# Routing of a mixture of experts, computed for each tile of 128 tokens by itself

## The chip, the core and the metric

The kernel runs on one core of a Trainium2 chip. The metric is device microseconds of that core for one execution; three executions of the kernel before are known, and one further execution was profiled. TensorE (PE) does the matmuls, VectorE (DVE) and ScalarE (ACT) the elementwise work, GpSimd (POOL) a little of it, and SyncE (SP) issues the loads. Each engine takes its instructions in the order in which the program lists them for it, and waits on semaphores for the others.

## What is computed

Two transformer layers over 256 tokens of width 1024, in float32. The change lies in the mixture of experts at the end of the second one. In the notation of the reference:

- the layer's output `x` is normed (`rms_norm`), then two routers give 8 group logits and 64 expert logits per token, each with a bias;
- the group with the largest logit is chosen, and in it the two experts with the largest logits; a token's weights are the softmax of the two, times the softmax probability of the group;
- each expert (64 of them, 256 hidden units: gate, up and down matrices) is applied to the tokens that chose it, and the weighted results are added to `x`.

## The kernel before

The 256 tokens lie in two tiles `t` of 128 (a token on each of 128 partitions). Instructions are written in Python; a scheduler then sets each engine's order by priority and by when it supposes that operands will be ready, and adds the semaphores. `streams` and `on` give a block of code a priority of its own: "route" ahead of "late".

**The end of the mixers.** `accum_end` (calls L946 for `x`) finishes `x[:, 0]`, then `x[:, 1]`, and calls `then(0)` shortly before the last matmuls of tile 1 and `then(1)` behind them. `then(t)` (L1687) squares and sums each half of x on ScalarE (L1694, into `q4`), transposes x on TensorE (`hT`, L1699, L1701), and splits x into `xhi` (ScalarE, L1704) and the remainder `xlo` (VectorE, L1685). `logits(t)` multiplies `hT` by the router's weights into `ps[0]`, 72 columns per tile: tile 0's logits are issued in `then(1)`, tile 1's at its end. Behind both, `rstd2` (L420 to L433) computes the norm factors `rs` of both tiles as one [128, 2] operand, and L1718, L1719 make the logits `lg` and `le`.

**The choice.** `route` (L1737) works on both tiles at once, with operands of 16 or 128 elements per partition: `first_max` (L1730 to L1734) three times for group, first and second expert, one-hot matrices `rA` and `rB` (L1757, L1759), whose matmuls with a triangular and an all-ones matrix count, for each token, how many tokens before it chose the same expert; `rk` (L1768) is this rank. From it `expert_gather` makes the 0/1 matrices S (L1816), and 32 matmuls of S with `xhi` and `xlo` gather the tokens of eight experts into `xT` (L1833, L1834). `weigh` (L1770) computes the weights behind that.

**Fillers.** `keep_warm` (L1658) issues WARM = 22 matmuls of two constants (shown as `mm<-negcr,identr`) behind tile 1's logits, at the priority "late"; their result is not used.

**Memory banks.** The matmuls' results lie in banks of PSUM, held by pools. The pool "ps1" of the mixers is closed (`psum.close()`, L1584) and "ps4" opened (L1586) ahead of `route`: the banks of the logits belong to the first, those of the fillers, of the ranks and of the experts to the second.

**The experts.** `moe` (L1914) goes through 16 groups of four experts. The weights come in 1 MB tiles into a ring of 16 buffers; `first_weights` (L1898) issues the first loads, before the routing, and `expert_ahead` (L1868) issues one whenever a buffer is freed, all from SP (L1883).

Of the kernel before, what the change touches and what calls it, by code (L numbers as in the profile page):

```python
# [149 lines left out]
class Kern:  # L150
# [1514 lines left out]
    def router_logits(self, x):  # L1665
# [6 lines left out]
        lg = self.T(16, "lg").rearrange("p (t g) -> p t g", t=2)  # L1672
        le = self.T(128, "le").rearrange("p (t e) -> p t e", t=2)
        q4 = self.T(4, "n4q4")
        rs, hr = (self.ph.tile([128, 2], F, name=k) for k in ("n4rs", "n4hr"))
        ps = []

        def logits(t):
            for k in range(8):
# [6 lines left out]

        def then(t):  # L1687
            if t == 0:
                ps.append(self.bank("sm"))
            else:  # L1690
                logits(0)
            for i in range(2):
                junk = self.T(512, "junk")
                nc.scalar.activation(junk, x[:, t, i * 512:i * 512 + 512], AF.Square, accum_out=q4[:, 2 * t + i:2 * t + i + 1])  # L1694
# [19 lines left out]
            logits(1)  # L1714
            for t in range(2):
                r = rs[:, t:t + 1]
                v = ps[0][:, t * 72:t * 72 + 72]
                nc.vector.scalar_tensor_tensor(lg[:, t], v[:, 0:8], r, self.b["b_router_group_2"], op0=OP.mult, op1=OP.add)  # L1718
                nc.vector.scalar_tensor_tensor(le[:, t], v[:, 8:72], r, self.b["b_router_expert_2"], op0=OP.mult, op1=OP.add)  # L1719
        self.rs4, self.hr4 = rs, hr  # L1720
        return (lg, le), (hi, lo), then

    def first_max(self, v, name):

        nc = self.nc
        mx, m2 = self.T(2, name + "m"), self.T(2, name + "n")
        e = self.T(16, name + "e").rearrange("p (t g) -> p t g", t=2)
        oh = self.T(16, name + "o").rearrange("p (t g) -> p t g", t=2)
        b = lambda t: t[:, :, None].to_broadcast([128, 2, 8])
        nc.vector.tensor_reduce(mx, v, axis=AX.X, op=OP.max)  # L1730
        for t in range(2):
            nc.vector.scalar_tensor_tensor(e[:, t], v[:, t], mx[:, t:t + 1], self.c["desc"], op0=OP.is_equal, op1=OP.mult)
        nc.vector.tensor_reduce(m2, e, axis=AX.X, op=OP.max)
        nc.vector.tensor_tensor(oh, e, b(m2), op=OP.is_equal)  # L1734
        return oh, mx

    def route(self, lg, le):  # L1737

        nc, c, mm = self.nc, self.c, self.nc.tensor.matmul
        b = lambda t, n=8: t[:, :, None].to_broadcast([128, 2, n])  # L1740
        f = lambda t: t.rearrange("p t g -> p (t g)")
        with self.on("late"):
            self.keep_warm(WARM, self.logit)
        ohg, mg = self.first_max(lg, "fg")
        d = self.T(16, "rd").rearrange("p (t g) -> p t g", t=2)
        nc.vector.tensor_tensor(d, lg, b(mg), op=OP.subtract)
        g4 = ohg[:, :, :, None].to_broadcast([128, 2, 8, 8])
        e4 = lambda t: t[:, :, None, :].to_broadcast([128, 2, 8, 8])
        v4 = lambda t: t.rearrange("p (t g e) -> p t g e", t=2, g=8)
        tmp = self.T(128, "rt")  # L1750
        nc.vector.tensor_tensor(v4(tmp), le.rearrange("p t (g e) -> p t g e", g=8), g4, op=OP.mult)
        el = self.T(16, "el").rearrange("p (t e) -> p t e", t=2)
        nc.vector.tensor_reduce(el, v4(tmp).rearrange("p t g e -> p t e g"), axis=AX.X, op=OP.add)
        o1, v1 = self.first_max(el, "f1")
        nc.vector.scalar_tensor_tensor(el, o1, BIG, el, op0=OP.mult, op1=OP.add)
        A1, A2 = self.T(128, "rA"), self.T(128, "rB")
        nc.vector.tensor_tensor(v4(A1), g4, e4(o1), op=OP.mult)  # L1757
        o2, v2 = self.first_max(el, "f2")
        nc.vector.tensor_tensor(v4(A2), g4, e4(o2), op=OP.mult)  # L1759
        self.rk = self.gs.tile([128, 2, 64], F, name="rk")  # L1760
        p = self.bank()
        for A in (A1, A2):
            mm(p[:, 0:128], c["stri"], A, start=A is A1, stop=False)
            mm(p[:, 64:128], c["ones"], A[:, 0:64], start=False, stop=A is A2)
        nc.vector.tensor_tensor(A1, A1, A2, op=OP.add)
        self.low()
        rk = self.rk.rearrange("p t e -> p (t e)")
        nc.vector.scalar_tensor_tensor(rk, p[:, :128], 1.0, A1, op0=OP.add, op1=OP.mult)  # L1768

        def weigh():  # L1770

            self.W = self.gs.tile([128, 2, 64], F, name="rW")
            e2, w1, pg = self.T(2, "e2"), self.T(2, "w1"), self.T(2, "pg")
            w = self.T(16, "aw").rearrange("p (t e) -> p t e", t=2)
# [3 lines left out]
            nc.vector.tensor_reduce(pg, d, axis=AX.X, op=OP.add)  # L1778
# [4 lines left out]
            nc.vector.tensor_tensor(w1, w1, self.rs4, op=OP.mult)  # L1783
# [356 lines left out]
```

## Time and profile before

| | us |
|---|---|
| median of three executions | 1461.39 (1459.74 to 1462.12) |
| the profiled execution, its own time | 1462.19 |
| its span in the profile | 1460.4 |
| TensorE busy | 1385.0 (95%) |
| VectorE busy | 864.1 (59%) |
| ScalarE busy | 588.9 (40%) |
| weight loads, mean over the span | 233 GB/s |

The span is counted from the first to the last instruction of the profiled execution; 1.8 us of its time lie around it. Engine shares are means over stages of different kind: the mixers and the first layer up to about 980 us, the routing from about 980 to 1001, and the experts from there. Rows of the timeline carry the start in the span, the busy time, the engine, the line, the operation, the tiles written and read, the size and the number of like instructions.

### The profile page before, as it was taken

The page shows a single profiled execution, that of the slowest core. Times are in us where ns is not written, and L with a number is a line of the kernel's source. Part 1 is how long each engine was busy: PE and PEld are TensorE (multiplying, and loading weights), DVE is VectorE, ACT ScalarE, POOL GpSimd, SP SyncE. Part 2 cuts the span into 40 slices and gives each one's busy share as a digit, 9 for nine tenths or more (in the row PEclk, how much of TensorE's full clock was granted, in tenths as well). Part 3 has the DMA queues.
Part 4 walks back from the last instruction along what each step waited for, and adds up shares of the span by engine and source line. Part 5 has one row for each costly group of instructions (what it writes and reads, how often), then busy time and mean ns, then how long its engine had stood idle before and what let it go on. Part 6 is the DMA issues. An engine that isn't in the chain of part 4 may idle for free.

```text
span 1460.4 us, 22493 instructions
## 1 busy us (share of the span) xinstructions
PE 1385.0 (95%) x9045; PEld 1052.3 (72%) x9045; DVE 864.1 (59%) x1750; ACT 588.9 (40%) x1062; POOL 91.9 (6%) x71
## 2 busy tenths in 40 slices
PE   7999999999999999899999999999999999999996
PEld 6989998999899999688798899985434333333321
DVE  7788686567788778588868886873213113112212
ACT  5546655544555556355664664451111001101100
POOL 0110202020011111200000000000000000000000
PEclk9999999999999999899999999998999999999999
DMA  8413423433555556433345345497999999999996
GB/s 272 146 60 118 145 75 104 154 107 124 191 170 182 196 178 198 124 117 115 103 130 172 90 142 173 149 388 322 422 421 421 421 421 420 421 421 420 421 421 274
DMA packets 132010, 341.32 MB, mean 234 GB/s; under 512 B 7872, under 2 KB 84672, under 8 KB 107840
## 3 DMA queue, kind: packets, MB, share of 16 engines
q1 hardware_dynamic: 131904, 339.86, 62.6%
q8 instruction: 72, 1.18, 0.3%
q14 instruction: 34, 0.28, 0.1%
HBM read 338.79 MB, written 1.05 MB: 233 GB/s over the span
## 4 chain that ended last, share of the span: by engine, by line
PE 72%; DMA 12%; DVE 10%; ACT 4%; issue 1%; POOL 0%; SPq 0%; DVEq 0%; ACTq 0%; POOLq 0%
PE mm L143 45%; PE sm L143 13%; PE at L143 6%; PE dn L143 5%; DMA raw<-in_wdn 4%; DMA early<-in_wdn 3%; DMA early<-in_wgu 2%; PE sm L147 2%; DVE whl L322 2%; DMA raw<-in_wgu 1%; ACT whl L321 1%; DMA raw<-in_w_in 1%; PE at L147 1%; ACT myhi L334 1%; DMA raw<-in_w_down 0%
## 5 line engine op out<-in xcount | busy, mean ns | idle before, releaser
L322 DVE TENSOR_TENSOR whl<-raw,whl 128x1024 fp32r<-128x1024 f32 (+2 forms) x256 | 306.0, 1198 | 80.4 <-ACT whl L321 78.8
L321 ACT ACTIVATE whl<-raw 128x1024 fp32r<-128x1024 f32 (+2 forms) x256 | 262.3, 1026 | 180.6 <-PE mm L143 155.7
L143 PE MATMUL mm<-raw,xT 128*32 128x512 f32 x672 | 184.1, 595 | 5.2 <-ACT xT L1833 2.8
L143 PE MATMUL mm<-n1hi,whl 128*128 128x256 f32 (+2 forms) x880 | 173.8, 289 | 0.0
L335 DVE SCALAR_TENSOR_TENSOR mylo<-dn,wq,myhi 128x512 fp32r<-128x512 f32 x32 | 24.0, 751 | 217.3 <-ACT myhi L334 215.7
L143 PEld LDWEIGHTS mm<-n1hi,whl 128*128 128x128 f32 (+2 forms) x880 | 140.2, 190 | 0.7 <-ACT n1hi L334 0.2
L143 PE MATMUL mm<-n3hi,whl 128*128 128x256 f32 (+1 forms) x656 | 127.3, 288 | 2.4 <-DVE whl L322 1.5
L143 PE MATMUL mm<-n2hi,whl 128*128 128x256 f32 x704 | 129.5, 285 | 0.1
L143 PE MATMUL mm<-n1lo,whl 128*128 128x256 f32 (+2 forms) x440 | 125.4, 285 | 1.0 <-DVE n1lo L335 1.0
L143 PEld LDWEIGHTS mm<-n2hi,whl 128*128 128x128 f32 x704 | 111.3, 193 | 0.7 <-ACT n2hi L334 0.3
L143 PEld LDWEIGHTS mm<-n3hi,whl 128*128 128x128 f32 (+1 forms) x656 | 103.5, 189 | 5.2 <-issue 2.0
L143 PEld LDWEIGHTS mm<-raw,xT 128*32 128x32 f32 x672 | 43.1, 109 | 83.7 <-issue 71.6
L334 ACT ACTIVATE myhi<-dn,wq 128x512 fp32r<-128x512 f32 x32 | 22.0, 688 | 198.5 <-PE dn L143 198.5
L143 PE MATMUL mm<-n2lo,whl 128*128 128x256 f32 x352 | 99.8, 285 | 0.3 <-DVE n2lo L335 0.3
L143 PE MATMUL dn<-raw,mhT 128*32 128x512 f32 x384 | 92.9, 594 | 2.7 <-DMA raw<-in_wdn 2.2
L143 PE MATMUL mm<-n3lo,whl 128*128 128x256 f32 (+1 forms) x328 | 93.6, 285 | 0.0
L143 PEld LDWEIGHTS mm<-n1lo,whl 128*128 128x128 f32 (+2 forms) x440 | 83.3, 189 | 1.8 <-DVE n1lo L335 1.4
L143 PEld LDWEIGHTS dn<-raw,mhT 128*32 128x32 f32 x384 | 26.4, 110 | 61.2 <-issue 52.5
L143 PEld LDWEIGHTS mm<-n2lo,whl 128*128 128x128 f32 x352 | 67.9, 193 | 0.9 <-DVE n2lo L335 0.5
L143 PE MATMUL mm<-whl,n3hi 128*128 128x512 f32 x192 | 61.2, 396 | 2.0 <-DVE whl L322 1.5
L143 PEld LDWEIGHTS mm<-n3lo,whl 128*128 128x128 f32 (+1 forms) x328 | 62.0, 189 | 1.0 <-issue 0.7
L143 PE MATMUL mm<-early,xT 128*32 128x512 f32 x144 | 61.3, 595 | 0.0
(536 smaller groups left out, 2719.7 us busy)
## 6 DMA issues: line engine op xcount, KB each, us to landing
raw<-in_wgu SPq DMA_DIRECT2D x84, 1024.0 KB, 19.8
raw<-in_w_in SPq DMA_DIRECT2D x56, 1024.0 KB, 5.3
raw<-in_wdn SPq DMA_DIRECT2D x48, 1024.0 KB, 19.8
whl<-in_wgu SPq DMA_DIRECT2D x26, 1024.0 KB, 19.8
raw<-in_w_up SPq DMA_DIRECT2D x22, 1024.0 KB, 5.1
early<-in_wgu SPq DMA_DIRECT2D x18, 1024.0 KB, 19.8
raw<-in_w_down SPq DMA_DIRECT2D x11, 1024.0 KB, 4.8
whl<-in_wdn SPq DMA_DIRECT2D x9, 1024.0 KB, 19.8
```

The lines of the kernel that those rows point to most:

```text
L143: return self.of.matmul(out, lhsT, rhs, **k)
L147: return self.of.transpose(*a, **k)
L321: nc.scalar.activation(out[0], w, AF.Copy)
L322: nc.vector.tensor_tensor(out[1], w, out[0].bitcast(F), op=OP.subtract)
L334: nc.scalar.activation(hi, src, AF.Copy, scale=scale)
L335: nc.vector.scalar_tensor_tensor(lo, src, scale, hi.bitcast(F), op0=OP.mult, op1=OP.subtract)
```

## The change

`route` is cut in two. `scale(t)` computes the norm factor of one tile: ten operations of one element per partition, called in `then(t)`. `route_part(t)` makes the logits, the three choices, the one-hots `A1` and `A2`, their matmuls and the rank of one tile: 21 operations of VectorE with 1, 8 or 64 elements per partition and two matmuls of 64 columns, for tile 0 two more (the all-ones matrix, which adds tile 0's counts to tile 1's ranks). `route_part(0)` is called in `then(1)` right behind `logits(0)`; `route_part(1)` is kept as `route_last` and called in `route`, behind the call of `keep_warm`. The bank `p` of the rank matmuls is now taken in `then(0)`, next to that of the logits, and so from the pool "ps1". The tiles that both parts write are held in `self.rt`; `weigh` takes over the subtraction that makes `rd`.

```diff
@@ block23
-            lgs, xs, then = self.router_logits(x)
+            xs, then = self.router_logits(x)
...
             with self.on("route"):
-                weigh = self.route(*lgs)
+                weigh = self.route()
@@ router_logits
+        def scale(t):
+            r, (v, h, w) = rs[:, t:t + 1], (self.T(1, "n4" + k) for k in "vhw")
+            nc.vector.tensor_tensor(v, q4[:, 2 * t:2 * t + 1], q4[:, 2 * t + 1:2 * t + 2], op=OP.add)
+            nc.vector.tensor_scalar(v, v, 1.0 / 1024, EPS, op0=OP.mult, op1=OP.add)
+            nc.vector.tensor_scalar(r.bitcast(I32), v.bitcast(I32), -0.5, MAGIC, op0=OP.mult, op1=OP.add)
+            nc.vector.tensor_scalar(h, v, -0.5, None, op0=OP.mult)
+            for _ in range(3):
+                nc.vector.scalar_tensor_tensor(w, r, h, r, op0=OP.mult, op1=OP.mult)
+                nc.vector.scalar_tensor_tensor(r, w, 1.5, r, op0=OP.add, op1=OP.mult)
...
             if t == 0:
-                ps.append(self.bank("sm"))
+                ps.extend(self.bank("sm") for _ in range(2))
             else:
                 logits(0)
+                self.route_part(0, *ps)
...
             if t == 0:
+                scale(0)
                 low(0, 0)
                 low(0, 1)
                 return
-            ssq = self.T(2, "n4q")
-            nc.vector.tensor_tensor(ssq, q4[:, 0:4:2], q4[:, 1:4:2], op=OP.add)
-            self.rstd2(ssq, "n4", rs)
+            scale(1)
             low(1, 0)
             self.low = lambda: low(1, 1)
             logits(1)
...
+            self.route_last = lambda: self.route_part(1, *ps)
@@ first_max
+    def first_max(self, v, oh, mx, name):
...
         nc.vector.tensor_reduce(mx, v, axis=AX.X, op=OP.max)
+        nc.vector.scalar_tensor_tensor(e, v, mx, self.c["desc"], op0=OP.is_equal, op1=OP.mult)
         nc.vector.tensor_reduce(m2, e, axis=AX.X, op=OP.max)
+        nc.vector.tensor_scalar(oh, e, m2, None, op0=OP.is_equal)
...
+    def route_part(self, t, ps, p):
...
+        nc.vector.scalar_tensor_tensor(lg, v[:, 0:8], r, self.b["b_router_group_2"], op0=OP.mult, op1=OP.add)
+        nc.vector.scalar_tensor_tensor(le, v[:, 8:72], r, self.b["b_router_expert_2"], op0=OP.mult, op1=OP.add)
+        self.first_max(lg, og, z["mg"][:, t], "fg")
+        tmp, el = self.T(64, "rt"), self.T(8, "el")
+        nc.vector.tensor_tensor(v4(tmp), v4(le), g4, op=OP.mult)
+        nc.vector.tensor_reduce(el, v4(tmp).rearrange("p g e -> p e g"), axis=AX.X, op=OP.add)
+        self.first_max(el, o1, z["v1"][:, t], "f1")
+        nc.vector.scalar_tensor_tensor(el, o1, BIG, el, op0=OP.mult, op1=OP.add)
+        nc.vector.tensor_tensor(v4(A1), g4, e4(o1), op=OP.mult)
+        self.first_max(el, o2, z["v2"][:, t], "f2")
+        nc.vector.tensor_tensor(v4(A2), g4, e4(o2), op=OP.mult)
+        for i, A in enumerate((A1, A2)):
+            mm(p[:, t * 64:t * 64 + 64], c["stri"], A, start=t == 0 and i == 0, stop=i == 1)
+        if t == 0:
+            for A in (A1, A2):
+                mm(p[:, 64:128], c["ones"], A, start=A is A1, stop=False)
+        s = self.T(64, "rs")
+        nc.vector.tensor_tensor(s, A1, A2, op=OP.add)
+        nc.vector.scalar_tensor_tensor(rk, p[:, t * 64:t * 64 + 64], 1.0, s, op0=OP.add, op1=OP.mult)
...
         with self.on("late"):
             self.keep_warm(WARM, self.logit)
...
+        self.route_last()
         self.low()
```

What the scheduler makes of it on TensorE, between tile 1's logits (`sm<-rw,h2T`) and the first gather matmul (`sm<-S,xhi`). `negcr,identr` are the fillers, `rA` and `rB` the one-hot matrices (in the changed program `rA_10452` is A1 and `rA_10453` is A2, of both tiles). Before:

```order
L143 MATMUL sm<-rw,h2T 128x72 x3
L143 MATMUL mm<-negcr,identr 128x128 [waits DVE_49,PE_49]
L143 MATMUL mm<-negcr,identr 128x128 x11
L143 MATMUL sm<-rA,consts 128x128 [waits DVE_49]
L143 MATMUL sm<-rA,consts 128x64
L143 MATMUL mm<-negcr,identr 128x128 x4
L143 MATMUL sm<-rB,consts 128x128 [waits DVE_49]
L143 MATMUL sm<-rB,consts 128x64
L143 MATMUL mm<-negcr,identr 128x128 x6
L143 MATMUL sm<-S,xhi 128x256 [waits DVE_49] x2
```

And in the changed kernel:

```order
L143 MATMUL sm<-rA_10452,consts 128x64 [waits DVE_49]
L143 MATMUL sm<-rA_10453,consts 128x64 [waits DVE_49]
L143 MATMUL sm<-rA_10452,consts 128x64
L143 MATMUL sm<-rA_10453,consts 128x64
L143 MATMUL sm<-rA_10452,consts 128x64 [waits DVE_49]
L143 MATMUL sm<-rA_10453,consts 128x64 [waits DVE_49]
L143 MATMUL mm<-negcr,identr 128x128 [waits DVE_49]
L143 MATMUL mm<-negcr,identr 128x128 x21
L143 MATMUL sm<-S,xhi 128x256
L143 MATMUL sm<-S,xhi 128x256 [waits DVE_49]
```

The fillers, which stood in three pieces ahead of, between and behind the one-hot matmuls, stand in one piece behind the last of them, and the first waits for VectorE.

On VectorE, the end of the norm factors and the logits before:

```order
L946 SCALAR_TENSOR_TENSOR x<-sm,x 128x512
L1685 TENSOR_TENSOR xlo<-x,xhi 128x512
L1710 TENSOR_TENSOR n4q<-n4q_10443 128x2
L420 TENSOR_SCALAR n4v<-n4q 128x2
L427 TENSOR_SCALAR n4rs<-n4v 128x2
L428 TENSOR_SCALAR n4h<-n4v 128x2
L432 SCALAR_TENSOR_TENSOR n4t<-n4rs,n4h 128x1 x2
L433 SCALAR_TENSOR_TENSOR n4rs<-n4t,n4rs 128x2
L1685 TENSOR_TENSOR xlo<-x,xhi 128x512
```

The same place in the changed kernel, from the last x (L946) into tile 0's choice; L1683 to L1689 are `scale`, L1736 to L1739 `first_max`, L1698 is `xlo`:

```order
L946 SCALAR_TENSOR_TENSOR x<-sm,x 128x512
L1751 SCALAR_TENSOR_TENSOR rlg<-sm,n4rs,rows 128x8
L1752 SCALAR_TENSOR_TENSOR rle<-sm,n4rs,rows 128x64
L1736 TENSOR_REDUCE rmg<-rlg 128x1
L1698 TENSOR_TENSOR xlo<-x,xhi 128x512
L1737 SCALAR_TENSOR_TENSOR fge<-rlg,rmg,consts 128x8
L1738 TENSOR_REDUCE fgn<-fge 128x1
L1739 TENSOR_SCALAR rog<-fge,fgn 128x8
L1755 TENSOR_TENSOR rt<-rle,rog 128x64
L1698 TENSOR_TENSOR xlo<-x,xhi 128x512
L1756 TENSOR_REDUCE el<-rt 128x8
```

Tile 0's logits and choice follow the last x directly, with both remaining `xlo` between them. The norm factor of tile 1 (L1683 to L1689) begins sixteen operations and two `xlo` behind the first `rlg` row, among the last steps of tile 0's chain; tile 1's own `rlg` stands behind tile 0's rank and half of S.

## Rows read from the trace of the kernel before

**Rows 1.** The page's part 2, bandwidth in 40 slices of 36.5 us each.
```profile
GB/s 272 146 60 118 145 75 104 154 107 124 191 170 182 196 178 198 124 117 115 103 130 172 90 142 173 149 388 322 422 421 421 421 421 420 421 421 420 421 421 274
```

**Rows 2.** Windows: busy time per engine, granted clock, DMA share, GB/s.
```profile
998.00:1000.00 2.00, 2.00 (x11) 2.00 (x11) 0.73 (x2) 0.55 (x2) 1.01 (x2) 0.50 0.90 369
1000.00:1002.00 2.00, 2.00 (x16) 1.49 (x16) 1.05 (x4) 0.91 (x2) 0.00 (x0) 0.99 0.11 41
...
1014.00:1016.00 2.00, 2.00 (x12) 0.47 (x8) 0.00 (x0) 0.00 (x0) 0.00 (x0) 1.00 0.39 82
...
1020.00:1040.00 20.00, 20.00 (x125) 9.86 (x126) 3.52 (x8) 3.57 (x7) 1.21 (x2) 1.00 1.01 423
```

**Rows 3.** Timeline of the load queue (SP): start us, us, line, op, transfer.
```profile
982.17 0.33 SPq L1883 DMA_DIRECT2D whl<-in_wdn  x1
1005.22 0.33 SPq L1883 DMA_DIRECT2D early<-in_wdn  x1
```

**Rows 4.** Timeline of TensorE, routing and gather (PE matmul, PEld weight load).
```profile
984.18 2.21 PE L143 MATMUL sm<-rw,h2T 128*128 128x72 f32 x16 [0.25 <-ACT h2T L1701]
...
988.62 1.73 PE L143 MATMUL mm<-negcr,identr 128*128 128x128 f32 x12 [2.23 <-DVE fgm L1730]
...
991.59 1.12 PE L143 MATMUL sm<-rA,consts 128*128 128x128 f32 x4 [1.25 <-DVE rA L1757]
...
994.10 1.40 PEld L143 LDWEIGHTS mm<-negcr,identr 128*128 128x128 f32 x6
...
995.38 0.55 PEld L143 LDWEIGHTS sm<-S,xhi 128*128 128x128 f32 x2
...
995.49 0.73 PE L143 MATMUL sm<-S,xhi 128*128 128x256 f32 x2
...
996.45 0.63 PE L143 MATMUL sm<-S,xhi 128*128 128x256 f32 x2
...
996.88 0.63 PE L143 MATMUL sm<-S,xlo 128*128 128x256 f32 x2
...
1000.89 0.40 PE L143 MATMUL sm<-S,xhi 128*128 128x256 f32 x2
...
1001.13 0.40 PE L143 MATMUL sm<-S,xlo 128*128 128x256 f32 x2
...
1001.57 2.77 PE L143 MATMUL mm<-early,xT 128*32 128x512 f32 x12
```

**Rows 5.** Timeline of VectorE and ScalarE in the same stretch; [idle before <-releaser].
```profile
980.67 0.69 DVE L946 SCALAR_TENSOR_TENSOR x<-sm,x 128x512 f32<-128x512 f32 x1 [2.24 <-PE sm L143]
...
982.48 0.68 DVE L946 SCALAR_TENSOR_TENSOR x<-sm,x 128x512 f32<-128x512 f32 x1
...
984.77 0.16 DVE L1710 TENSOR_TENSOR n4q<-n4q 128x2 f32<-128x2 f32 x1 [1.00 <-ACT junk L1694]
...
985.11 0.63 ACT L1704 ACTIVATE xhi<-x 128x512 fp32r<-128x512 f32 x1
...
985.90 0.69 DVE L1685 TENSOR_TENSOR xlo<-x,xhi 128x512 fp32r<-128x512 f32 x1
986.50 0.34 DVE L432 SCALAR_TENSOR_TENSOR n4t<-n4rs,n4h 128x1 f32<-128x1 f32 x2
...
988.98 0.17 DVE L1733 TENSOR_REDUCE fgn<-fge 128x2 f32<-128x16 f32 x1
989.18 0.18 DVE L1734 TENSOR_TENSOR fgo<-fge,fgn 128x16 f32<-128x16 f32 x1
...
994.45 0.29 DVE L1768 SCALAR_TENSOR_TENSOR rk<-sm,rA 128x128 f32<-128x128 f32 x1 [1.30 <-PE sm L143]
994.77 0.76 DVE L1816 TENSOR_TENSOR S<-rk,consts 128x256 fp32r<-128x256 f32 x2
```

**Rows 6.** Windows of 0.25 us, columns as in rows 2; granted clock third from last.
```profile
989.75:990.00 0.25, 0.25 (x4) 0.25 (x3) 0.25 (x1) 0.00 (x0) 0.00 (x0) 0.58 1.28 524
...
1000.00:1000.25 0.25, 0.25 (x4) 0.25 (x3) 0.24 (x1) 0.00 (x0) 0.00 (x0) 0.94 0.16 66
```

More of the change, by code (lines that the diff above doesn't have):

```diff
@@ L1671, in router_logits @@
         hi, lo = v(self.U8("xhi", R)), v(self.U8("xlo", R))
-        lg = self.T(16, "lg").rearrange("p (t g) -> p t g", t=2)
-        le = self.T(128, "le").rearrange("p (t e) -> p t e", t=2)
         q4 = self.T(4, "n4q4")
@@ L1676, in router_logits @@
         ps = []
+        two = lambda n, name: self.ph.tile([128, 2 * n], F, name=name).rearrange("p (t g) -> p t g", t=2)
+        z = self.rt = {k: two(n, "r" + k) for k, n in (("lg", 8), ("le", 64), ("og", 8), ("o1", 8), ("o2", 8), ("mg", 1),
+                                                      ("v1", 1), ("v2", 1), ("A1", 64), ("A2", 64), ("rk", 64))}
+        self.rk = z["rk"]
+        def scale(t):
[7 more added lines that the diff above has]
+                nc.vector.scalar_tensor_tensor(r, w, 1.5, r, op0=OP.add, op1=OP.mult)
         def logits(t):
@@ L1714, in then @@
             logits(1)
[L1715 to L1719, printed above, removed]
+            self.route_last = lambda: self.route_part(1, *ps)
         self.rs4, self.hr4 = rs, hr
-        return (lg, le), (hi, lo), then
@@ L1723, in first_max @@
-    def first_max(self, v, name):
+        return (hi, lo), then
+    def first_max(self, v, oh, mx, name):
         nc = self.nc
[L1726 to L1729, printed above, removed]
+        m2, e = self.T(1, name + "n"), self.T(8, name + "e")
         nc.vector.tensor_reduce(mx, v, axis=AX.X, op=OP.max)
-        for t in range(2):
-            nc.vector.scalar_tensor_tensor(e[:, t], v[:, t], mx[:, t:t + 1], self.c["desc"], op0=OP.is_equal, op1=OP.mult)
+        nc.vector.scalar_tensor_tensor(e, v, mx, self.c["desc"], op0=OP.is_equal, op1=OP.mult)
@@ L1733, in first_max @@
         nc.vector.tensor_reduce(m2, e, axis=AX.X, op=OP.max)
[L1734 to L1740, printed above, removed]
+        nc.vector.tensor_scalar(oh, e, m2, None, op0=OP.is_equal)
+    def route_part(self, t, ps, p):
+        nc, c, mm, z = self.nc, self.c, self.nc.tensor.matmul, self.rt
+        r = self.rs4[:, t:t + 1]
+        v = ps[:, t * 72:t * 72 + 72]
+        lg, le, og, o1, o2 = (z[k][:, t] for k in ("lg", "le", "og", "o1", "o2"))
+        A1, A2, rk = (z[k][:, t] for k in ("A1", "A2", "rk"))
+        g4 = og[:, :, None].to_broadcast([128, 8, 8])
+        e4 = lambda o: o[:, None, :].to_broadcast([128, 8, 8])
+        v4 = lambda o: o.rearrange("p (g e) -> p g e", g=8)
+        nc.vector.scalar_tensor_tensor(lg, v[:, 0:8], r, self.b["b_router_group_2"], op0=OP.mult, op1=OP.add)
[17 more added lines that the diff above has]
+        nc.vector.scalar_tensor_tensor(rk, p[:, t * 64:t * 64 + 64], 1.0, s, op0=OP.add, op1=OP.mult)
@@ L1741, in route @@
+    def route(self):
+        nc, z = self.nc, self.rt
+        b = lambda t, n=8: t.to_broadcast([128, 2, n])
         f = lambda t: t.rearrange("p t g -> p (t g)")
+        g4 = z["og"][:, :, :, None].to_broadcast([128, 2, 8, 8])
+        e4 = lambda t: t[:, :, None, :].to_broadcast([128, 2, 8, 8])
+        o1, o2, v1, v2 = (z[k] for k in ("o1", "o2", "v1", "v2"))
         with self.on("late"):
             self.keep_warm(WARM, self.logit)
-        ohg, mg = self.first_max(lg, "fg")
-        d = self.T(16, "rd").rearrange("p (t g) -> p t g", t=2)
@@ L1746, in route @@
[L1746 to L1764, printed above, removed]
@@ L1765, in route @@
-        nc.vector.tensor_tensor(A1, A1, A2, op=OP.add)
+        self.route_last()
         self.low()
-        rk = self.rk.rearrange("p t e -> p (t e)")
-        nc.vector.scalar_tensor_tensor(rk, p[:, :128], 1.0, A1, op0=OP.add, op1=OP.mult)
         def weigh():
             self.W = self.gs.tile([128, 2, 64], F, name="rW")
-            e2, w1, pg = self.T(2, "e2"), self.T(2, "w1"), self.T(2, "pg")
-            w = self.T(16, "aw").rearrange("p (t e) -> p t e", t=2)
+            e2, w1, pg = (self.T(2, k).rearrange("p (t o) -> p t o", t=2) for k in ("e2", "w1", "pg"))
+            w, d = (self.T(16, k).rearrange("p (t e) -> p t e", t=2) for k in ("aw", "rd"))
+            nc.vector.tensor_tensor(d, z["lg"], b(z["mg"]), op=OP.subtract)
@@ L1777, in weigh @@
             nc.scalar.activation(e2, v2, AF.Exp)
-            nc.vector.tensor_reduce(pg, d, axis=AX.X, op=OP.add)
+            nc.vector.tensor_reduce(pg[:, :, 0], d, axis=AX.X, op=OP.add)
             nc.vector.reciprocal(pg, pg)
@@ L1782, in weigh @@
             nc.vector.tensor_tensor(w1, w1, pg, op=OP.mult)
-            nc.vector.tensor_tensor(w1, w1, self.rs4, op=OP.mult)
+            nc.vector.tensor_tensor(w1[:, :, 0], w1[:, :, 0], self.rs4, op=OP.mult)
             nc.vector.tensor_scalar(self.hr4, self.rs4, 0.5, None, op0=OP.mult)
```

## The prediction

> **What bounds the kernel now.** I read the span in slices first. From the slice that begins at 1022 us on the weight DMAs move 420 to 422 GB/s without a break [rows 1], and the window of 20 us at 1020 shows all 16 DMA engines busy, share 1.01 [rows 2]. So the last 430 us (the mixture of experts, 200 MB of expert weights) run at the pace of the weight stream, and the kernel ends a fixed time after the stream last stood still. The 2 us windows show where that is: share 0.90 at 998 and 0.11 at 1000, then a shorter rest at 1014, share 0.39 [rows 2]. The queue of weight loads shows why: the load issued at 982.17 fills the last free buffer, and the next one goes out at 1005.22, as soon as TensorE has used up the first expert tile [rows 3]. TensorE's first expert matmul starts at 1001.57 [rows 4]. **Hence the rule of the whole forecast: whatever moves the first expert matmul moves the restart of the stream, and with it the end, by the same amount**, later without limit, earlier by at most the 5 us from 1000.2 to 1005.2 in which the stream rests.
>
> Ahead of that matmul stands the routing. Tile 1's logits run on TensorE from 984.18 for 2.21 us [rows 4]; VectorE computes the norm factors for both tiles from 984.77, then the choice of groups and experts, the rank `rk` at 994.45 and the gather matrices S from 994.77 [rows 5]; the gather's matmuls start at 995.49, its last pair at 1001.13 [rows 4]. Two other things share this stretch. TensorE has little to do, so the program gives it 22 filler matmuls; in the trace 12 run from 988.62, 4 between the one-hot matmuls, 6 from 994.10, all while VectorE still works, so that they cost nothing [rows 4]. And TensorE's clock falls: half of the granted clock (1.2 of 2.4 GHz) from about 989.8 (0.58 in the window at 989.75), full again only at 1000.0 [rows 6], although TensorE was at work since 991.59 [rows 4]; the filler and one-hot matmuls of 991.6 to 995.4 did not bring it back, and it came 4.5 us after the gather had begun.
>
> **Part one: VectorE's chain.** The change makes two chains of one, each for 128 tokens. The price of a step is 0.20 us, since the 0.17 us L1733 at 988.98 is followed by its reader at 989.18 [rows 5]; halving an operation's 16 or 128 elements hardly lowers it. What matters is when tile 0's chain can run. Its first ten operations (norm factor) fall into VectorE's idle time: nine of them, 1.8 us, against an idle 2.24 us ahead of 980.67 [rows 5]. They begin only when the squares are summed, so I charge 0.3 us, by which the later x of tile 1 (issued at 982.48 and 0.68 long before [rows 5]) ends at 983.5. Tile 0's routing follows from there. One chain from `lg` to `rk` is 21 operations: 4.2 us; two are 8.4. Between them stand tile 1's ten norm operations, four of which fit into gaps of tile 0's chain, so 1.2; two `xlo` at 0.60 of issue, 1.2 (0.69 long, the next starts at 986.50 [rows 5]); the first half of S, 0.4 (half of the 0.76 of L1816 [rows 5]). The second of these `xlo` stands in the middle of tile 0's chain and needs the last `xhi`, which ScalarE ends at 985.74 [rows 5]; the chain gets there about 985.5, so 0.3 of waiting. The two ranks wait for their one-hot matmuls: the before kernel's `rk` waited 1.30 for four passes of them [rows 5], two passes of half the width are wanted now, and I take 0.4 each. Six operations need no earlier result and start 0.1 sooner: minus 0.6. Sum: 983.5 + 8.4 + 1.2 + 1.2 + 0.4 + 0.3 + 0.8 - 0.6 = 995.2. Against 994.45 **the last rank comes 0.7 us later**, not earlier; bounds 994.7 (no waits) to 995.9 (a 1.3 us wait at the second rank). The reason is plain: tile 1's sums are ready at 984.77 [rows 5], but VectorE, which takes its work in order, is with tile 0 until about 989.5.
>
> **Part two: the fillers.** TensorE also works in order, and all 22 fillers now stand between the last one-hot matmul and the gather, the first with a wait on VectorE. Their bank belongs to a pool that is opened where the old one is closed; the change leaves the last read of the old pool, tile 1's `rk`, behind that point, and the awaited count in the built program is that operation. So no filler can run while VectorE works; they all run when it is done. Their pace at half clock is 1.28 us for the six from 994.10 to the gather's first weight load at 995.38 [rows 4], 0.213 each; 22 take 4.7 us. The clock is low by then: TensorE has some six short matmuls between the logits' end at 986.39 and 995. The first filler starts at 995.2 + 0.3 (the length of `rk` and a handover), S is ready 0.4 later and hidden. **The gather starts at 995.5 + 4.7 = 1000.2, 4.7 us later than 995.49.**
>
> **Part three: the gather.** It has 32 matmuls, 0.43 a pair at half clock (996.45 to 996.88) and 0.24 a pair at full clock (1000.89 to 1001.13) [rows 4]. Before, from 995.49 to the first expert matmul at 1001.57, it took 6.1 with the clock back after 4.5 us. Where the clock returns in the new gather can't be read from the trace. If it is back 2 us into it, 9 matmuls are slow and 23 fast, 4.7 us in all and 5.0 to the first expert matmul (1.1 less than before); if it stays low to the end, 32 x 0.213 = 6.8, or 7.1 (1.0 more). I take 0.3 less, since fillers run right before it; the end at 7.1 is unlikely because the clock would have to stay low for 11 us of continuous work, against 8.4 from 991.59 to 1000.0, so I keep +0.5 as the upper end.
>
> **Part four: the rest.** The weights of the pair of experts (`weigh`) get one more subtraction in the shadow of the gather; two one-hot matmuls of 64 columns for tile 0 run while TensorE idles; ScalarE's and the load queue's orders stay; the memset of `base` moves into an early idle place. All zero: TensorE or the stream is what is waited for. If the `weigh` chain lost its cover, it would be 0.2.
>
> **Sum.** +4.7 - 0.3 = +4.4 us on the first expert matmul, bounds: rank at 994.7 and gather 1.1 shorter, +3.1; rank at 995.9 and gather 0.5 longer, +5.9. The profiled execution (span 1460.4, its own time 1462.19) would become 1466.6; it lies 0.8 above the median of the three runs, so on the median of 1461.39 the forecast is **1465.8**. About 0.2%, 2.9 us, is what a measurement of this kernel can tell from no change.
>
> **Rivals.** *A, the clock comes back during the fillers.* 22 matmuls in a row are work, too. If it returns as the gather begins, the gather takes 16 x 0.24 + 0.3 = 4.1 instead of 6.1, and the sum is +2.7: 1464.1. If it returns half-way through the fillers, 11 of them save 0.1 each: +1.6, 1463.0. Against it: 3.9 us of fillers and one-hots, from 991.59, did not do it before [rows 4, 6]. The Trainium skill speaks for it: "TensorE: Matmul & The Clock Gate", What's actually happening, says that "the default state is throttled, and activity releases the throttle". By that rule 22 unbroken matmuls would end in the full clock, and rival A's time would hold; no row of before shows such a run of fillers alone.
>
> *B, not slower: the clock does not fall at all.* If TensorE's few one-hot matmuls of tile 0, about 987.8 to 989.3, keep the clock up, the fillers take between half of 0.213 and the 1.73 / 12 = 0.144 of the twelve from 988.62 [rows 4], 2.4 to 3.2 us, and the gather 4.1: first expert matmul at 995.5 + 2.4 + 4.1 = 1002.0 to 1002.8, +0.4 to +1.2, 1461.8 to 1462.6, which is no change. It decides if the clock is full at 995.5. Against it: before, it fell at 989.8 although twelve fillers had been running since 988.62 [rows 4, 6]; now the gap is longer and emptier.
>
> *C, the stream takes the delay up.* If the restart hung on something else than the first tile's release, the delay would vanish in the stream: 0, or 1461.4. (If only the second short rest shrank, 1.2 us in the window at 1014 [rows 2], 3.2 would be left, inside the forecast's own range.) Against it: the load at 1005.22 goes out right behind TensorE's use of that tile [rows 3, 4], and that second rest comes from TensorE's steps too, so it moves along.
>
> *D, faster, as the change is meant.* If tile 0's chain were done by 984.77, tile 1's own part, ten and 21 operations or about 6.4 us, would put the rank at 991.2, 3.3 us earlier; with the fillers at half clock behind it the gather would still start at 996.2, 0.7 late. Only if the clock holds as well, as in B, does it start at 993.9 and the first expert matmul at 998.0: -3.6, 1457.8. Tile 0's x is complete on VectorE only about 983 [rows 5], so I give it little.
>
> **Chances.** Forecast 0.78; A 0.10; B 0.05; C 0.04; D 0.03. A to C lie within 0.2%, D is faster with the clock up; of the forecast's own range all lies above +2.9. So slower 0.78, same 0.19, faster 0.03. The range runs from 1463.0 (most of A is inside; B, C and D are not) to 1467.3 (+5.9); some 0.14 is left out.
>
> **What would show it.** Right: in the changed profile no filler runs between 986.5 and 995; `rk` of tile 1 ends about 995.4; 22 fillers in a row about 995.5 to 1000.2 at a granted clock of 0.50; gather from about 1000.2; first expert matmul about 1006; the stream rests about 1000 to 1010.5 and runs at 421 GB/s from there, with all later stages shifted. Wrong in part one if the last rank ends before 994; wrong in part two if fillers run at full clock or before the rank; wrong in the rule if the first expert matmul moves and the end does not.

## The result

The changed kernel takes 1467.95 us (median of 6 runs, 1465.47 to 1469.61), the kernel before 1460.38 beside it (6 runs, 1457.37 to 1462.12). The ratio is 1.0055, 95% interval 1.0044 to 1.0066: **8.0 us slower (6.4 to 9.6)**. The forecast was slower by 4.4, with a range up to 1467.3. The direction was right, the size too small.

The profiled execution took 1469.15 us with a span of 1467.4, against 1460.4 before: 7.0 us in the traces. How far a run has come when the routing begins differs from run to run (the row of VectorE that completes tile 0's `x`, L946 x2, called the last joint x here, starts at 977.06 before, 977.38 after, between 973.25 and 977.83 in the experiments), so from here on times are also given from the start of that x.

TensorE of the changed kernel, from tile 0's one-hot matmuls to the first expert matmul. Columns of a timeline: start, duration (us), engine, line, operation, output and inputs, count, and in brackets the idle time ahead and what ended it.

```profile
989.33 1.54 PE L143 MATMUL sm<-rA,consts 128*128 128x64 f32 x6 [0.62 <-DVE rA L1761]
995.22 0.69 PE L143 MATMUL sm<-rA,consts 128*128 128x64 f32 x2 [4.36 <-DVE rA L1759]
996.28 0.69 PE L143 MATMUL sm<-rA,consts 128*128 128x64 f32 x2 [0.37 <-DVE rA L1761]
997.28 4.96 PE L143 MATMUL mm<-negcr,identr 128*128 128x128 f32 x22 [0.32 <-DVE rrk L1769]
1002.04 0.73 PE L143 MATMUL sm<-S,xhi 128*128 128x256 f32 x2
...
1008.05 1.48 PE L143 MATMUL mm<-early,xT 128*32 128x512 f32 x6
```

All 22 fillers stand in one piece behind tile 1's rank and hold up the gather by 1002.04 - 997.28 = 4.76 us. It begins at 1002.04 (before 995.49), the first expert matmul at 1008.05 (1001.57) [rows 4]. VectorE, with the waits that matter:

```profile
983.68 0.22 DVE L1751 SCALAR_TENSOR_TENSOR rlg<-sm,n4rs,rows 128x8 f32<-128x8 f32 x1
...
986.09 0.69 DVE L1698 TENSOR_TENSOR xlo<-x,xhi 128x512 fp32r<-128x512 f32 x1 [0.47 <-ACT xhi L1718]
...
990.90 0.23 DVE L1769 SCALAR_TENSOR_TENSOR rrk<-sm,rs 128x64 f32<-128x64 f32 x1 [1.05 <-PE sm L143]
...
992.14 0.23 DVE L1751 SCALAR_TENSOR_TENSOR rlg<-sm,n4rs,rows 128x8 f32<-128x8 f32 x1
...
992.66 0.23 DVE L1737 SCALAR_TENSOR_TENSOR fge<-rlg,rmg,consts 128x8 f32<-128x8 f32 x1
992.92 0.16 DVE L1738 TENSOR_REDUCE fgn<-fge 128x1 f32<-128x8 f32 x1
993.12 0.23 DVE L1739 TENSOR_SCALAR rog<-fge,fgn 128x8 f32<-128x8 f32 x1
993.39 0.22 DVE L1755 TENSOR_TENSOR rt<-rle,rog 128x64 f32<-128x64 f32 x1
...
997.00 0.23 DVE L1769 SCALAR_TENSOR_TENSOR rrk<-sm,rs 128x64 f32<-128x64 f32 x1 [0.52 <-PE sm L143]
```

Tile 0's rank (the first `rrk`) waits 1.05 us for the six one-hot passes of 989.33, and tile 1's norm factor stands behind it, so tile 1's `rlg` comes only at 992.14. Tile 1's rank comes at 997.00, where `rk` stood at 994.45 [rows 5]. The queue of weight loads and the DMA engines in windows (columns: window, length, busy time of PE, PEld, DVE, ACT, POOL, granted clock, DMA share, GB/s):

```profile
982.37 0.33 SPq L1898 DMA_DIRECT2D whl<-in_wdn  x1
1011.70 0.33 SPq L1898 DMA_DIRECT2D early<-in_wdn  x1
```

```profile
1000.00:1002.00 2.00, 2.00 (x11) 2.00 (x11) 0.00 (x0) 0.00 (x0) 1.19 (x2) 0.50 0.13 53
1010.00:1012.00 2.00, 2.00 (x12) 0.53 (x10) 0.00 (x0) 0.00 (x0) 0.61 (x1) 1.00 0.00 0
1014.00:1016.00 2.00, 2.00 (x15) 1.08 (x12) 0.00 (x0) 0.27 (x1) 0.00 (x0) 1.00 1.02 430
...
989.25:989.50 0.25, 0.17 (x1) 0.18 (x2) 0.25 (x5) 0.00 (x0) 0.00 (x0) 0.65 1.18 492
...
1006.25:1006.50 0.25, 0.25 (x3) 0.25 (x3) 0.20 (x1) 0.02 (x1) 0.00 (x0) 0.71 0.00 0
```

The load that went out at 1005.22 [rows 3] now goes out at 1011.70; the stream has run dry at 1000, as before [rows 2], and rests 6.5 us longer. The clock is at half (0.50) from about 989.3 to 1006.4, through all the fillers, and returns 4.4 us after the gather began.

### The profile page after: what moved, and what is told of

Read it like the earlier page. It is cut to its first block, busy times and chain, and to the rows that moved or that the text cites. A ratio compares the mean times of both kernels' runs of the same rounds, so it can differ in the third digit from the quotient of the medians.

```text
span 1467.4 us, 22519 instructions
## 1 busy us (share of the span) xinstructions
PE 1388.0 (95%) x9049; PEld 1054.7 (72%) x9049; DVE 865.7 (59%) x1773; ACT 588.1 (40%) x1062; POOL 93.1 (6%) x71
## 3 DMA queue, kind: packets, MB, share of 16 engines
HBM read 338.79 MB, written 1.05 MB: 232 GB/s over the span
## 4 chain that ended last, share of the span: by engine, by line
PE 72%; DMA 11%; DVE 10%; ACT 4%; issue 1%; POOL 1%; SPq 0%; DVEq 0%; ACTq 0%; POOLq 0%
PE mm L143 45%; PE sm L143 14%; DMA raw<-in_wdn 7%; PE at L143 6%; PE dn L143 5%; DMA early<-in_wgu 2%; PE sm L147 2%; DVE whl L322 2%; DMA raw<-in_wgu 1%; ACT whl L321 1%; DMA raw<-in_w_in 1%; PE at L147 1%; ACT myhi L334 1%; POOL fy L1152 0%; DVE pr L478 0%
```

## The experiments

Every kernel below ran five rounds beside the kernel before. One table holds what was read from the traces (us from the start of the last joint x, one execution each; "gather lasts" is up to the first expert matmul; "restart" is the load behind the first expert tile) and the times (ratio to before times 1460).

| kernel | last rank | gather starts | gather lasts | restart | time against before, us |
|---|---|---|---|---|---|
| before | 17.39 | 18.43 | 6.08 | 28.16 | 0 |
| after | 19.62 | 24.66 | 6.01 | 34.32 | +8.0 (6.4 to 9.6) |
| e1: after, no fillers | 18.96 | 19.24 | 5.84 | 28.73 | +2.5 (1.2 to 3.8) |
| e2: after, bank of tile 1's rank from the new pool | 19.47 | 21.15 | 5.94 | 30.74 | +4.2 (2.9 to 5.5) |
| e3: before, bank of `rk` from the old pool | 16.89 | 21.99 | 6.10 | 31.74 | +3.7 (2.3 to 5.0) |
| e4: before, no fillers | 16.89 | 17.69 | 6.49 | 27.83 | -0.4 (-1.8 to +1.0) |
| e5: before, wide fillers | 16.48 | 17.29 | 4.14 | 25.08 | -2.0 (-3.4 to -0.7) |
| e6: after, tile 0's rank later | 18.82 | 23.85 | 6.35 | 33.85 | +8.6 (6.6 to 10.7) |
| e7: before, norm factor by tile | 16.63 | 17.67 | 6.04 | 27.36 | +0.3 (-1.0 to +1.6) |
| e8: e5 and e7 together | 15.71 | 16.51 | 4.13 | 24.29 | -3.5 (-5.0 to -1.9) |
| e9: e6 with 24 wide fillers | 18.57 | 18.84 | 5.56 | 28.05 | +0.7 (-1.0 to +2.3) |
| e10: e6 with 29 wide fillers | 18.59 | 18.87 | 5.63 | 28.15 | +0.3 (-1.2 to +1.8) |

Theory at the start: the loss is the fillers behind tile 1's rank plus a longer VectorE chain, and the restart of the stream hands it to the end. Rivals: the clock, or the chain alone.

**e1, the fillers out of the changed kernel.**

```diff
-            self.keep_warm(WARM, self.logit)
+            self.keep_warm(0, self.logit)
```

> The changed kernel without its 22 filler matmuls. Theory F (the loss is first of all the 22 fillers, which queue behind tile 1's rank, 4.76 us in the changed profile): the gather starts 0.5 us behind tile 1's rank, about 997.7 instead of 1002.04, and the kernel loses only the longer VectorE chain, about 2.2 us, plus up to 1.0 if the clock stays at half through the whole gather: 2.0 to 3.3 us over before. Rival K (the loss is the clock, which the fillers win back): the gather takes 7 us instead of 6 and little is gained, 5.5 us or more over before. Rival M (the program behind the routing has become slower): still 7 over before.

1462.81 us against 1460.39, ratio 1.0017 (1.0008 to 1.0026). Two rows of VectorE and the gather's first:

```profile
989.48 0.23 DVE L1769 SCALAR_TENSOR_TENSOR rrk<-sm,rs 128x64 f32<-128x64 f32 x1 [0.39 <-PE sm L143]
995.58 0.23 DVE L1769 SCALAR_TENSOR_TENSOR rrk<-sm,rs 128x64 f32<-128x64 f32 x1 [0.53 <-PE sm L143]
```

```profile
995.86 1.04 PE L143 MATMUL sm<-S,xhi 128*128 128x256 f32 x3 [0.32 <-DVE rrk L1769]
```

The gather starts 0.28 after the rank instead of 5.04, and 5.6 us of the restart's 6.2 are gone. What stays is the longer chain: the last rank comes 1.57 later than before; a gather that starts closer behind it (0.28 against 1.04) and is 0.24 shorter gives 1.0 of this back, so the restart is 0.6 late. The time is 2.5 later (1.2 to 3.8), more than the restart explains. In this execution the one-hot passes of tile 0 still fell into the full clock (0.88 for six, 1.54 in the changed kernel), so the first rank waited 0.39 and not 1.05.

**e2, the fillers set free another way.** Tile 1's rank takes its bank from the pool that is opened later; the all-ones passes move there with it. The last read of the old pool is then that of tile 1's logits, for which the fillers still wait.

```diff
+        if t == 1:
+            p = self.bank()
+            for i, A in enumerate((z["A1"][:, 0], z["A2"][:, 0])):
+                mm(p[:, 64:128], c["ones"], A, start=i == 0, stop=False)
```

> The changed kernel with tile 1's rank in a bank of the new pool, so that the fillers wait only for tile 1's logits to be read; they stand 9, 4 and 9 between the one-hot matmuls. F: the fillers are hidden again, the gather starts about 0.5 us behind tile 1's rank, and the time is 2 to 2.5 us over before. K: clock granted at half from 990 to the middle of the gather as in both kernels, no gain over the kernel without fillers. M: 7 over before. If F and K both fall short, something else holds the gather back.

1463.87, ratio 1.0029 (1.0020 to 1.0038). The fillers now run in pieces of 9, 4 and 9, the first two while VectorE works; some of the last piece still stands ahead of the gather:

```profile
992.89 2.16 PE L143 MATMUL mm<-negcr,identr 128*128 128x128 f32 x9
...
994.85 0.73 PE L143 MATMUL sm<-S,xhi 128*128 128x256 f32 x2
```

Tile 1's rank was at 993.17 and half of S had long been there, so the gather could have begun about 993.5 and began at 994.85. The wait came from the pool, and giving the last reader another bank takes most of it away (1.68 behind the rank instead of 5.04). Two things fell short of the 2 to 2.5 us that were expected: this rest of the fillers, and a second rank that waited 0.97, with fillers between its one-hot passes, where it waits 0.52 in the changed kernel.

**e3, the wait alone, in the kernel before.**

```diff
-                ps.append(self.bank("sm"))
+                ps.extend(self.bank("sm") for _ in range(2))
+                self.rank_bank = ps[1]
...
-        p = self.bank()
+        p = self.rank_bank
```

> The kernel before with one thing changed: the bank of the rank matmuls is taken from the old pool, so that all 22 fillers stand behind the rank, as in the changed kernel; VectorE's work is untouched. F: rank as before or a little earlier (its one-hot matmuls no longer share TensorE with fillers, up to 0.4), then 22 x 0.216 = 4.75 us of fillers, gather from about 999.3, 4.0 to 4.8 us over before. Rival V (VectorE's two chains are the loss): no loss here.

1462.88, ratio 1.0025 (1.0016 to 1.0034). TensorE:

```profile
993.54 4.96 PE L143 MATMUL mm<-negcr,identr 128*128 128x128 f32 x22 [0.38 <-DVE rk L1769]
998.29 0.73 PE L143 MATMUL sm<-S,xhi 128*128 128x256 f32 x2
```

The routing is that of before, word for word; where a bank comes from is enough to push all fillers behind `rk` and to cost 3.6 us at the restart and 3.7 in the time. The same 4.75 us lie between the first filler and the gather. About 0.5 of it is paid back at the rank (16.89 against 17.39), because the one-hot passes no longer share TensorE with fillers.

**e4, no fillers in the kernel before.** The edit is that of e1.

> The kernel before without fillers: what they are worth where they cost nothing. F: the gather starts as before or up to 0.4 earlier; the time is between 0.4 less and 1.0 more than before. K: the clock comes back later than at 1000.0, the gather takes 6.8 to 7.1 instead of 6.1 us, and the time is 0.7 to 1.0 more.

1460.06, ratio 0.9997 (0.9988 to 1.0007). The rank comes 0.5 earlier, the gather lasts 0.4 longer. The fillers of the kernel before gain nothing that can be measured; the clock falls and returns with or without them.

**e5, fillers that TensorE can run at once.** The narrow ones are taken out and 22 matmuls of 512 columns go behind tile 1's logits, on a bank of the old pool.

```diff
+        def hold(n):
+            p = self.bank("mm")
+            for _ in range(n):
+                nc.tensor.matmul(p[:, 0:512], self.identr, hi[:, 0, 0:512], start=True, stop=True)
...
             logits(1)
+            hold(22)
```

> The kernel before with its 22 fillers of 128 columns taken out and 22 matmuls of 512 columns put in, from a bank of the old PSUM pool, so that nothing makes them wait: two inside the second tile's logits, twenty behind them and ahead of the one-hots. They fill TensorE's idle time from the logits' end to the first one-hot, 5.3 us in the kernel before without fillers, at about 0.22 each (17 matmuls of 512 columns of the first expert took 4.05). Theory: the clock stays full when TensorE has no gap, the narrow fillers of before only come too late and too sparse. Then the four passes of each one-hot take 0.55 instead of 1.1, `rk` waits 0.3 instead of 0.81, and the gather takes 4.1 to 4.5 instead of 6.08 to 6.49: 1.5 to 2.5 us faster than before. Rival: the clock falls whatever stands there, or in the gap between the one-hots and the gather, and returns 3.7 to 4.6 us after the gather's start as in all kernels so far: within 0.5 us of before.

1457.09 against 1459.03, ratio 0.9986 (0.9977 to 0.9995): faster than before. TensorE and one window:

```profile
986.25 4.90 PE L143 MATMUL mm<-xhi,identr 128*128 128x512 f32 x20
991.53 0.63 PE L143 MATMUL sm<-rA,consts 128*128 128x128 f32 x4 [0.37 <-DVE f2m L1736]
992.66 0.66 PE L143 MATMUL sm<-rB,consts 128*128 128x128 f32 x4 [0.50 <-DVE rB L1765]
994.16 0.74 PE L143 MATMUL sm<-S,xhi 128*128 128x256 f32 x4 [0.84 <-DVE S L1822]
```

```profile
993.00:994.00 1.00, 0.32 (x4) 0.18 (x2) 0.61 (x3) 0.00 (x0) 0.00 (x0) 1.00 0.98 410
```

The granted clock stays at 1.00 throughout. The one-hot passes take 0.63 instead of 1.1, the rank waits 0.35, and the gather takes 4.14, within 0.04 of what the prediction's rival A reckoned for a gather at full clock.

**e6, the wait of tile 0's rank taken off the path.** In the changed kernel, fillers and all, tile 0's sum and rank are issued behind tile 1's `rle`.

```diff
+        last = nc.vector.scalar_tensor_tensor(le, v[:, 8:72], r, ...)
+        if t == 1:
+            with self.tc.issue_after(last.ins):
+                self.rank_of(0, p)
```

> The kernel after, with tile 0's sum and rank issued behind tile 1's `rle` on VectorE instead of in the middle of tile 1's norm factor; TensorE's order is not changed, the 22 fillers stay behind tile 1's rank. Theory: the first rank's wait of 1.05 us for the six one-hot passes lies wholly on the path, because tile 1's norm factor stands behind it on VectorE; without it tile 1's rank comes 18.5 to 18.7 us after the last joint x instead of 19.62, and the kernel is about 1.0 us faster than after (about 7.0 slower than before). Rival: the wait is given back at the second rank, which then waits for its own one-hots or for something else; then less than 0.4 us is gained.

1467.45, ratio 1.0059 (1.0045 to 1.0073): not to be told from the changed kernel. The two ranks:

```profile
988.56 0.23 DVE L1779 SCALAR_TENSOR_TENSOR rrk<-sm,rs 128x64 f32<-128x64 f32 x1
...
993.25 0.22 DVE L1779 SCALAR_TENSOR_TENSOR rrk<-sm,rs 128x64 f32<-128x64 f32 x1 [0.52 <-PE sm L143]
```

The wait of 1.05 is gone and the last rank comes 0.80 earlier, a little less than expected; 0.34 is given back by a gather of 6.35 instead of 6.01, since the clock returned later in it. The restart gains 0.47. So the wait did lie on the path, but a gain of that size is below what the times can show.

**e7, the part of the change that used idle time, alone.** `scale(0)` and `scale(1)` in the kernel before; everything from the logits on stays joint.

```diff
             if t == 0:
+                scale(0)
...
-            self.rstd2(ssq, "n4", rs)
+            scale(1)
```

> The kernel before, with only the norm factor taken per tile as the change does it (tile 0's ten operations in VectorE's idle time ahead of tile 1's x); logits, choice, one-hots and ranks stay joint, and the fillers stay where before has them. Theory: this part alone is a small gain: tile 1's steps by 128x1 take 0.22 where the pair takes 0.35, three times, so `rk` comes 0.3 to 0.5 us earlier, 16.9 to 17.1 us after the last joint x instead of 17.39; the time is 0.1 to 0.5 us below before's, at the edge of what can be measured. The loss of the change is then in the rest, the chains of choice run twice. Rival: the later x of tile 1, which comes some 0.2 later behind tile 0's operations, gives the gain back: within 0.2 us of before.

1459.94 against 1459.03, ratio 1.0002 (0.9993 to 1.0011). In the trace rank, gather and restart all come 0.76 to 0.80 earlier, more than expected; in the time nothing shows. The trace and the interval (down to -1.0) can both be right; alone, this run settles nothing.

**e8, e5 and e7 together.** With 20 wide matmuls, since the one-hots come earlier.

```diff
             if t == 0:
+                scale(0)
...
+            scale(1)
...
             logits(1)
+            hold(20)
```

> The wide fillers behind the second tile's logits (20 now) and the norm factor per tile in one kernel, everything else as in before. Theory: the two gains are in series on the path, so they add: `rk` 15.7 us after the last joint x (16.48 with the wide fillers alone, 16.63 with the norm factor alone, 17.39 in before), the expert's restart of the weight stream 24.3 us after it (25.08, 27.36 and 28.16), and the time 2.5 to 3.5 us under before's. Rival: an earlier restart no longer pays, because the stream behind it is bound by something else; the norm factor alone brought the restart 0.8 forward and no measurable time. Then the time equals that of the wide fillers alone, about 2.0 under before's, although the restart comes earlier.

1456.89 against 1460.77, ratio 0.9976 (0.9966 to 0.9987): **3.5 us faster than before (1.9 to 5.0) and faster than both kernels of this study.** Rank 15.71 and restart 24.29 are the expected values to 0.02. The two gains add in the trace. That the earlier restart still pays beyond e5 is likely but not shown, since the intervals of the two times overlap. What is left of the stream's rest in this trace:

```profile
999.00:1000.00 1.00, 1.00 (x8) 0.28 (x6) 0.00 (x0) 0.00 (x0) 0.32 (x1) 1.00 0.22 90
1000.00:1001.00 1.00, 1.00 (x6) 0.23 (x4) 0.00 (x0) 0.00 (x0) 0.00 (x0) 1.00 0.04 16
1001.00:1002.00 1.00, 1.00 (x8) 0.30 (x6) 0.00 (x0) 0.00 (x0) 0.00 (x0) 1.00 0.92 123
```

Two microseconds with little traffic: the traffic ends at about 999.2, 23.1 after the x, and 0.6 to 0.7 us lie between the load's issue at 1000.41 and the next traffic, so a restart much earlier than 22.4 (an estimate from these rows) would find the stream still running.

**e9 and e10, the order of the change with wide fillers.** e6 without the narrow fillers; e10 has `hold(29)` in the place of `hold(24)`.

```diff
-            self.keep_warm(WARM, self.logit)
+            self.keep_warm(0, self.logit)
...
             logits(1)
+            hold(24)
```

> The kernel after with tile 0's rank behind tile 1's `rle`, its 22 narrow fillers taken out, and 24 matmuls of 512 columns from the old PSUM pool around the one-hots, so that TensorE has work from the logits to tile 1's one-hots and the clock can stay full. What is left of the change is the order alone: two chains of choice on VectorE in place of one. Theory: the chain then still costs 1.9 to 2.3 us at the rank against the kernel with joint routing and wide fillers (rank 18.4 to 18.7 us after the last joint x against 16.48), of which 0.5 comes back because the gather finds half of S ready: restart about 26.6 after that x against 25.08 there and 28.16 in before, time 0.5 to 1.5 us under before's and 0.5 to 2 above the joint kernel with wide fillers. Rival: the change's loss was the fillers and the clock alone; with both gone the per-tile order is as fast as the joint one, restart within 0.5 us of 25.08. Or the clock falls in spite of the wide matmuls: restart then at 28.0 or later and no gain on before.

> The kernel after with tile 0's rank late and wide matmuls, as in the run before it, with 29 instead of 24 of them: there TensorE stood idle for 1.40 us ahead of tile 1's first one-hot, the granted clock fell at that place and the gather took 5.36 us. Five more at 0.235 fill 1.2 us of it. Theory: that gap was the cause; the clock stays full, the gather takes 4.1 to 4.4, the first rank waits no longer, the restart comes 26.8 to 27.1 us after the last joint x instead of 28.05 (before 28.16, joint routing with wide fillers 25.08 and, with the norm factor by tile, 24.29), and the time is 0.5 to 1.5 us under before's. What then is left against the joint order, 1.7 to 2.0 us at the restart, is the price of two chains of choice in place of one. Rival: the clock falls all the same, since the passes of 64 columns between the wide matmuls and the gather leave TensorE idle half of the time; then the restart stays at 28.0.

1461.17, ratio 1.0005 (0.9993 to 1.0016), and 1460.22, ratio 1.0002 (0.9992 to 1.0012). The expected rank was met (18.57 and 18.59), the expected clock was not, and the restarts (28.05 and 28.15) are those of the rivals. The 5.36 for the gather of e9 in the second text should be 5.56. In e9 TensorE idled 1.40 us ahead of tile 1's first one-hot; e10 filled that, and the clock fell all the same, as the rival said:

```profile
991.65 0.43 PE L143 MATMUL sm<-rA,consts 128*128 128x64 f32 x2 [0.25 <-DVE rA L1768]
992.70 0.43 PE L143 MATMUL sm<-rA,consts 128*128 128x64 f32 x2 [0.62 <-DVE rA L1770]
993.46 1.29 PE L143 MATMUL sm<-S,xhi 128*128 128x256 f32 x5 [0.32 <-DVE rrk L1785]
```

```profile
993.00:994.00 1.00, 0.68 (x5) 0.55 (x4) 0.79 (x5) 0.02 (x1) 0.00 (x0) 0.83 1.06 442
```

So the gap of e9 was not the cause, or not the only one. Why the clock held in e5 and e8 through a stretch that looks alike (one-hots and waits from 991.5 to 994.2) and fell here at about 993.7 is open. Apart from the clock these two runs price the order itself: with wide fillers the last rank comes 2.1 us later than in e5 and 2.9 later than in e8, the gather starts 1.6 and 2.3 later (half of S being ready gives 0.5 back).

## Why the prediction was right in direction and too small

*What bounds, and the rule.* Right in the traces: from the first expert matmul to the restart it is 3.65 us in all twelve, and from the restart to the end of the span 454.3 to 456.0. Times follow the restart over 10 us of shift in both directions (e8 to after). For seven of the eleven kernels the restart's shift against before lies inside the interval of the time. For the four that have the order of the change with narrow fillers or none (after, e1, e2, e6) the time lies 1.6 to 2.9 us above that shift, each outside its interval. Every trace is one execution; what makes up that difference is open.

*Part one, VectorE's chain.* **The step that failed.** Forecast: last rank 0.7 later, at most 1.5. Measured: 997.00 - 0.32 (the run's later x) - 994.45 = 2.2 later, beyond the bound. (Its bounds do not follow from its terms: without the waits the sum is 994.1, with 1.3 at the second rank 996.1, not 994.7 and 995.9; the measured 996.7 lies beyond either.) The start was right: 983.5 forecast for tile 0's `rlg`, 983.68 - 0.32 = 983.4 measured. From there 11.7 us were forecast and 13.3 taken:

- Waits, 0.9 more. The first rank waited 1.05 instead of 0.4. It waits for all six passes of that bank, the all-ones ones too, and they fell into the half clock. The `xlo` waited 0.47 instead of 0.3, the second rank 0.52 instead of 0.4. The prediction had two passes in mind for each rank. The upper bound held a 1.3 us wait at the second rank, and took it for granted that the first could not cost more than the 0.4.
- Price of a step, 0.7 more, nearly all of it in tile 1's chain, which takes 4.12 from its `rlg` to the sum ahead of the rank; 19 steps at 0.20, less 0.3 for early starts, were to make 3.5. 0.20 was read from one pair of rows [rows 5]. It holds for reductions of 8 elements (992.92 to 993.12), but the operations that take a scalar per partition cost 0.26 to 0.27 to the next reader (992.66 to 992.92, 993.12 to 993.39), which makes 0.4 of the 0.6. A chain has six of these, `first_max` making two each time; in the joint kernel one of each pair was a plain TENSOR_TENSOR at 0.21. Operations on 64 elements cost 0.25 to 0.31 and make the other 0.2. Rows of the changed kernel; L1688 has a scalar per partition and costs 0.26, L1689 has none and costs 0.19:

```profile
980.17 0.22 DVE L1688 SCALAR_TENSOR_TENSOR n4w<-n4rs,n4h 128x1 f32<-128x1 f32 x1
980.43 0.16 DVE L1689 SCALAR_TENSOR_TENSOR n4rs<-n4w,n4rs 128x1 f32<-128x1 f32 x1
980.62 0.22 DVE L1688 SCALAR_TENSOR_TENSOR n4w<-n4rs,n4h 128x1 f32<-128x1 f32 x1
...
993.64 0.27 DVE L1756 TENSOR_REDUCE el<-rt 128x8 f32<-128x64 f32 x1
993.95 0.16 DVE L1736 TENSOR_REDUCE rv<-el 128x1 f32<-128x8 f32 x1
...
996.00 0.22 DVE L1761 TENSOR_TENSOR rA<-rog,ro 128x64 f32<-128x64 f32 x1
996.26 0.23 DVE L1768 TENSOR_TENSOR rs<-rA,rA 128x64 f32<-128x64 f32 x1
```

The joint chain of the kernel before takes 5.13 for the same stretch:

```profile
987.73 0.23 DVE L1718 SCALAR_TENSOR_TENSOR lg<-sm,n4rs,rows 128x8 f32<-128x8 f32 x1
...
992.86 0.29 DVE L1765 TENSOR_TENSOR rA<-rA,rB 128x128 f32<-128x128 f32 x1
```

e1 (0.39 of waiting, last rank 0.66 earlier) and e6 (no wait, 0.80 earlier) show the first item; the second is read from rows only. In e1's execution the first rank waited as forecast, because its passes ran before the clock fell; its last rank was still 1.57 late. That halving an operation saves little was right: `rt` takes 0.22 with 64 elements and 0.29 with 128. The Trainium skill, "VectorE: DVE Perf Modes", The TRN2 errata, says that the latency is exposed between instructions, so that many small tiles pay it for each tile; the rows agree. e9 and e10 show the price of the whole order, 2.1 us at the rank with the long waits gone.

*Part two, the fillers.* Right: 22 fillers in one piece behind tile 1's rank, 4.7 us forecast, 4.76 measured, S hidden behind them. e1, e2 and e3 show the cause: taken out, given another bank, or the bank's origin alone.

*Part three, the gather.* 0.3 less was forecast, 0.07 less was measured (6.01); inside its bounds.

*Part four, the rest.* Nothing to see up to the restart, as forecast.

*The sum.* Forecast +4.4. At the restart it is +4.4 + 1.5 (part one) + 0.2 (part three) = +6.2, as measured (34.32 - 28.16). With 0.3 from the run's later x and 0.5 between restart and end this is the 7.0 of the spans; the runs' ratio says 8.0 (6.4 to 9.6). So part one alone takes the restart to the forecast's upper +5.9 and, with part three, past it; some 1.8 us of the time come on top that the restart does not show, and their cause is open.

*The rivals.* A fell: 22 fillers in a row at half clock, and the clock came back only 4.4 us into the gather (4.5 in before). The rule of the Trainium skill that was cited for it ("TensorE: Matmul & The Clock Gate", What's actually happening: activity releases the throttle) would have had the clock back at the end of the fillers, and the trace does not agree: the window at 1006.25 is the first above half. What pays is a clock that never falls (e5). B fell: half clock from 989.3. C fell: the restart took the whole delay. D fell: VectorE reached tile 1's `rlg` at 992.14. The reason given against it misreads a row: the x that is complete about 983 is tile 1's, while tile 0's is complete at 978.4 (977.06 + 1.37); ahead of tile 0's `rlg` stand that later x on VectorE and tile 0's logits on TensorE, which end at 983.4 in the changed kernel:

```profile
981.47 1.90 PE L143 MATMUL sm<-rw,h2T 128*128 128x72 f32 x16
```

D's idea has a true part, the norm factor of tile 0 in VectorE's idle time (e7, e8), and this is worth 0.8 at the restart.

## What to carry to other kernels

Work that is put ahead of other work on an in-order engine helps only if it ends before the other's inputs are ready. Cutting a chain of small operations in two halves gives two chains that are each nearly as long (here 4.1 us for tile 1's, 5.1 for the joint one), so move only the part that fits into idle time (here ten norm operations, not the choice). Ask of each moved buffer which pool it comes from: here one late reader of the closing pool held back the first work of the next one, with no data in common. And a matmul that is to keep the clock up must at least be placed where nothing makes it wait (e5, e8); that this is not always enough e9 and e10 show, so read the granted clock in the windows and not the program's intent.

## What was not expected of the hardware

- Fillers gained nothing that can be measured where the kernel before has them (e4), and other fillers 2.0 us where nothing makes them wait (e5). The half clock had cost the kernel before 2 us in the gather (6.08 against 4.14) and 0.4 at the last rank (16.89 in e4, 16.48 in e5) all along.
- Once down, the clock came back 3.3 to 5.4 us after the gather began in every kernel in which it fell, whatever stood ahead of it: nothing (e4), 22 fillers in a row (after, e3), or pieces of them (before, e2).
- A VectorE operation on 1 or 8 elements with a scalar per partition costs 0.26 to 0.27 us to its reader, one without 0.19 to 0.20.
